# One issue order replaced by another: a 24,000-operation trunk with the list of its order and of its buffer slots drawn up anew

## The chip, the cores and the metric

One core of a Trainium2 chip. The metric is the device time of one execution in microseconds (us); shown are the median of three runs and one profiled execution. Five instruction streams matter: TensorE (PE: matmuls and transposes; PEld is its weight load), VectorE (DVE), ScalarE (ACT), GpSimd (POOL) and SyncE (SP, which issues the DMAs). Each takes its own instructions strictly in the order in which they were written, and a semaphore holds it where it needs another stream's result.

## The reference

One decoder layer on 2048 tokens of width 1024: a gated delta-rule mixer in chunks with 8 heads and 4 heads of cross-attention on 256 memory rows, an output projection, and a squared-ReLU MLP, each followed by a scaled residual and a layer norm.

```python
proj = x @ w_in                                   # q, k, v, z, a, b, mq
qkv = silu(causal_depthwise_conv(qkv, conv_w))
o = chunk_gated_delta_rule(l2_normalize(q), l2_normalize(k), v, g, beta)   # needs inv(I + lower) per chunk
o = rms_norm(o, gate_norm_w) * silu(z)
mix = concatenate([o, memory_attention(mq, mem_k, mem_v)]) @ w_out
x = layer_norm(ALPHA * x + mix, ln1_g, ln1_b)
x = layer_norm(ALPHA * x + square(relu(x @ w_ff1)) @ w_ff2, ln2_g, ln2_b)
```

## The kernel before

The tokens go in four blocks of 512, two blocks to a superblock. For each block `mixer` runs the eight heads: `dense` projects q, k and v (tiles `aq`, `ak`, `av` in PSUM, 128x512, 24 matmuls each, because every product is made of three fp32r products of high and low halves), applies convolution and SiLU; `gate` does z (`az`); `gdn_a` builds the decay matrices, inverts the unit triangular matrices (`invert`) and scales v; `gdn_b` runs the recurrence over four chunks of 128 (`pc`, `po`). The memory heads are `amq`, `sps`, `pmT`, `pmo`. After two blocks comes the output projection `out_seven` (`ao`), then `ff1` (`fA`, `fB`, `fC`) and `ff2` (`f2A`, `f2B`, `f2C`). These three are built as seven products of half matrices instead of eight, and stream their weights through `wraw` and `whl`. Between the superblocks stands `gate_seven` (`az` again). The large matmuls are fp32r; the small ones of `invert` and of the recurrence, and the transposes, are fp32.

The recorder `rec` collects 23,792 operations of all five engines as the code names them. `Recorder.issue` then writes them out in the order of the table `ORDER` (one list for all engines, kept compressed), and gives each buffer of eleven tags the physical place that the table `SLOT` names. So these two tables alone decide what stands ahead of what on each engine, and which earlier buffer a new one must wait for.

Three places of the code are spoken of below. The first is the end of `invert` and what follows it in `gdn_a`: PE multiplies `pp`, DVE and then ACT copy its two halves into `Y`, and PE transposes v into the same PSUM bank (`ptv`).

```python
pq = bank("pq", "ga%d" % par)[:, :P].rearrange("p (c f) -> p c f", c=2)        # from LP and YP
nc.scalar.copy(out=Q.rearrange("p (c f) -> p c f", c=2), in_=pq)               # "inv<-pq"
pp = bank("pp", "ga%d" % par)[:, :P].rearrange("p (c f) -> p c f", c=2)        # from X64 and Q
nc.vector.tensor_scalar_mul(Y3[:64, 2:4, 64:], pp[64:], -1.0)                  # DVE "Y<-pp"
nc.scalar.activation(Y3[:64, 0:2, 64:], pp[:64], AF.Copy, scale=-1.0)          # ACT "Y<-pp"
pv = trans(v3, "ptv")                                                          # PE, same bank
```

The second is the input of that `pp`: the tiles `inv` (X64, LB, LP and others in four fixed buffers), which DVE, ACT and POOL fill with small copies, while POOL also makes `dl` and `at` from `gb` by two `affine_select` of 128x512. The third is in `out_seven`: ACT copies the first product out of PSUM (`e<-ao`), and only then may PE use that bank again.

Of the kernel before, what the change touches and what calls it, by code (L numbers as in the profile page):

```python
# [10 lines left out]
AF = mybir.ActivationFunctionType  # L11
# [3 lines left out]
P = 128  # L15
TB = 512
NC = TB // P
D = 1024
KT = D // P
H = 8  # L20
MH = 4
M = 256
# [149 lines left out]
class Op:  # L172
# [4 lines left out]
    "c-oYm4YKPvj;uFiM~MIA{x|lRUxJiRbxpsS=$X2<k1R_R2?B{kV$AgUw*CL(8J}+&pS1rs_uJ36fAnsBzH|TcP5G0`r+m`ff6dSHNnM}z{Av3y"  # L177
    "{n3~Av1NSf(($?P|K@#c$)A1Dx9yYd&%UYDeYk$0mi=kdo0PMDpnblJzwICDb^r1CWIobGjL&}i&BbTlKmY8@YWv`<|D^p}`{;e#K5I&xB0c;w"
    "_L)Zc)P1VV&FJ_xKOC_?NKg4>UGP4<`ipv*_JxdnMLK$4@uzoP?%3lp+a89#U+g#g3q@yYX}_v#`uqFsK5^59)=&Qw-C3!1kLNyBF8VQk;`xk+"
    "0s1D!OkZ!l(mmAr!P1IHpne)(9{N8WwV%`eq__QBJTpG)ysTBnmd1nSgSpRA_aN{)&wfJt_`08b;nYRfUiJ`GeO&k73&&R-yH8V#hGsvJI`lg_"  # L180
    "8H2uWMAxo|oA)^jv!?Fh*`vGv_0N{&A<G(^tT$<ocG}+^%sOVt{xt84&-+2><j;Po$NL#sC)n4aSy6{CwXFSSpC~;V0L`%eY3oxoF>CF<65g%m"
    "+t)AEyhpF;ay4$cw~y{}-@yL*p0yggwa$-g=IgFCV{+3&+y9s2^`5l6*iSSkX3qZWqcbK=+p3w^bW3|B<jz`{e4>~7XK}vN{Wfd3-WN${<rnm&"
    "^^X^2zs|{L`uTW|P2M-S=M_(GU%O7#8C|Ud4j!H-k7oHEr+shz(fk`M@T^%n*Qe^v_tk53^jT)r?yH`jXIXP_pFTgn>aL|wpY<AveTZ&QPj&YA"
    "(mqf3xA*Pom-Nu{im8+v$LM+NKVxBZqs5kFf1dk#XSj?_yYJ)LzGYuR;a>NU=WTNIG*cQeeN!xxvX9kz-G?+k87+$3_eEs=eV?31wtus-bTktC"
    "ekPBEIpYT@%cl>EjF-kF#z)t&&sg;HWj5xw4%<UkY;Q17W#4HjF%WSpd9O=;RU^2ELUU6`R31!{jnTd6Yo%*NWQ^#3uCgxsBC;oR;X1YnsqrYE"
    "SU%?x_Y>C$=%0rV_VsJ@WIy-3Zmj60=P>v0l)~6OT18s(`~O+UMW#YFgEe0E1J)G7ChH`R|Bz(Ba?z*LlVoo&I<xnheGXaQZA<sn=&|bQY69ul"
    "to772V)4K4+&_u+({f~>FtR?a|0mme<|z+B&zRrdmPw|d$?|C->#wrw8uxGJS?zhctrli^&+DvbwC_b`pzOKcyni)K`K*nlY0ujm9Jct;Y-S8F"
    "Xu7SmO+e8c+CQ&tpwxRS|Ng&yxAXUHPRz@F0WvkL@wTs6L$G9=mj|(*<Lmq%PhGfZ7K|)Fm$}-j#G{_H>~*1icJAoYWxe}i57y-JFtZ))jjCvU"
    "?q{bZT3Lg8I_zhN3$Pg4z2ES2`RB>BV?(su#=nn%cTpMhEUW%$n)5BJ)o5WKI+m;1GBj-odz?l-3sO%?2k4p`TaWCO+?T>XdzAC~{Z$st|L%WY"
    "Ph~&kGMBfS{Uf*`OdL-nxi-AjE`Wj3Eir}m5EpGCgYjtF3d&j(ycgN3rrZ8z=6#7xeH$*1SHb4-VLzXj^!Kr2tYn9@X7?_rd9wd4T(EZS_h!F3"  # L190
    "#{biDSnLIT4_4Q`<(1_KZaX8>RktzGcelmCHIxmJsm%Y|fg4>u#iMh|TJO=&Y}3Tlx$0g(C2@L<!1lkiqPC;A_cylJul`v~(7NvR??L41c-H$w"
    "4@bAEJzb-XD_KW;TP}d+{des9>+;s*)9H;aVIMeI^4n$X?<Z-Sox()Z647;X9{qjUrx<?5dZ%&Tj%^C7@H5n!6U>u^|EUvJ?O42h^jzgO6#dvX"
    "QCd^_Z0)JOv?n#q`MMXuVikL@)$65O&<jnYCOfJ(t>Df!KCy$Faqy}=MC}4aenDaj{PKERiS9)x)37&jnaI78+3NJcn$<7Lo+@pIv0rups(lR|"
    "u)W>AI+HxVSoCe5t1aE`UO5XVEnM&!rcT%5Ek6}I2fER=H<6CXk|F7M`!n1C?sc&_J+htoGnq3B_ge1jzDhl1ztf?a1LY>kJAO1pc#B)9Smx2}"
    "h>uu8#cw-?PH%Nk;-Kn>oU3nn&uw=2l;ViLFPm;RMrhyJU~}wU^AMA!lQbWm2zT_ieH9vYyB<APe;}_|-_n*pyo&QDeyZRk<aIwSE8(UUY+&LK"
    "`(d-Z%08mALuw?329!&ded4IKKbri)zM`S!@n}kC&AC+Md+%GR6L<KV|7>1ko3y<(Y5o)~rP7`_>6f9`9qtF)2fx+j(&LXkT_N7&scDd&;ZK)m"
    "eX?0t3Ie-b3VqK9j6LCHKYYD<;PZ(uYYR+XU+0v1*_aIS?z=V$9kc(;mozb-y%KWOv)PL#E_L5(BMR6fJsir(+&|j+DgmrEw?|<Po0)tuO?p|O"
    "rFo`3Y9H=V(!kZO<-FbzSaA_Uqu#j3!FRMO_Iev0ORcd-t65j3xhQ9KPp)helyDUJ-Bhp`*bJ;;VGFKuBM1qKLg$aJY_UpL_9`7VpwnL_BI2fG"
    "JBwC;ew`Df<K1Y#kr^c7?=l^u@#ERs5Vq!hyIPIw^B3#AT1{{5U8NGVmDmoy`o|mM7#L8Q8hLNL?fZWE)4b#CDVXKkXl`_dzTxT0<Zt_d!;mzo"
    "VjI}o^RPuNL^d2sw68~B{R?~cDTtN*!ZKz3n!*I_ZN-ti=I2U&*4}aXZGEfrV?|@Iw<Ol^o{4&DTAYh`HLSd@D{<N-BeRcPngW`oj82jT-Ih_K"  # L200
    "ptZ7(8neddEO@yaT_>p6G{Tk7)IU>pRJ%93@c!u~>>=$(B@3dz3N+B*wewcyM~|WEQ4i+279vMfZ5@Pii3yh;J;J>R?R{)BLL9;_rb9hCx|_ZS"
    "xX<aZm5_yZpHBSvotdTdkvA%f$-wMKyzDXWPgf;S#GuRoTx2SB8T-;Ik24ea>XtR69EIQ7v}%?SkE&&)uuOxw<e9WRq7}qS;Wujp?4+~fJm=&U"
    "&}pwHxxhFcMRs)m_>#x8fVlRsG)3N;N-~|LD8|r=l3yVoJn0D#;Fa+E`aWUbvm;|)Yau)(vftyf#}qgAt9Yh^lB~dY?v}M0wrJtq%Tdu|X~`ye"
    "+fr>?y5qg8R=(O78{IyB>5pu1YXl^t=iRXyOyad~M}evaLVp?oziflBWR3wy<}@n9L0YSNu6e}x?Sp05bTvHnm5shJT^mCdKdc9}M^?*QD^d?$"
    "b3oUsGgJZ=JsyRf^8fVtSK)$OAw9^i4YP(4OQ=|->w;5a+@?1vjW+|IaLD$4qj~YwcI%&$o!lEZ*riac?PPTVDOQ-~2p(H^xUT)Cf+;QmWy>Rs"
    "BRDJD^#HR>`|DMPAl2jT&AXjGnxcaVo8@+f-!dLQEDe8S%GegP>SOMU<h8m@B#?mK7OkhOJ7`ZpWp<nl(Q>AgKr5D<OPQA*1F3kb0~kE9K`k5^"
    "9G3a#@5F%F@8q-S#S+Hw$W`z7FuLt3>pQpEnh&;eo0S}kjT2}?{>*wpdYivTR!L6zUWF6Op-`$%Z-hxdKKALR-{EnMZ3rAGI&9n%6ELfTt&U6p"
    "tP>BAmuzI@#D3aL2sw;0#8dBkeOEjU#Zw*7^GO(B2B0gD*Q9>mEL)DghXTNld9&}Hiy5HY!#6ng44I&%aT8--=)@Aqhr<ikEVi`<>6I-5P!s0K"
    "Mk{ml)ijpvZ8JMqVZ98^iWPf+oy6F)_MccU_MEDnv5y9H|MKG(bI%=Fc5Ijc5p8OFW$)|OQyzP^tj9i*-tFhL_t15~u)UC{w)%Zh0Nwy>dtTQ*"
    "0@2uZqK?3=nq#tkMSGTLo@?RgV_DL#PNciT{@?54C)pK}=YqgvnQ87+AGAkdLF~_3*!zVcj(z^T1F3C)wEp#GU99DQ3l=OK8Gn0Uxt5f+ISpHT"  # L210
# [336 lines left out]

SLOT = {
    ("sp", "iv"): (
        "30212130130223103102213002312130"  # L550
    ),
    ("tp", "tt"): (
        "0246135702173546413650274310657201345210670514637240153647023165743061470265730154761243754052367150"
# [1661 lines left out]
```

## Time and profile before

| | us |
|---|---|
| median of 3 runs (lowest to highest) | 2703.33 (2702.78 to 2704.77) |
| profiled execution, its own time | 2706.16 |
| its span, first to last instruction | 2704.4 |
| PE busy | 2686.8 |
| DVE busy | 2152.1 |
| ACT busy | 1645.0 |
| POOL busy | 392.4 |

The profiled execution is 2.8 us above the median and 1.8 us above its own span. "Busy" of PE is the time in which at least one matmul record is open; records overlap, so PE counts as busy through a wait that is shorter than the tail of the record before it. Starts are therefore read where spacings matter. Names are those of the program with buffer numbers left out; since all recorded operations are written out by one call, they all carry line L678 (L700 in the changed kernel, whose tables are 22 lines longer).

### The profile page before, as it was taken

How to read it: one execution, taken by the hardware profiler on the slowest of the kernel's cores; microseconds unless marked ns; L12 is line 12 of the kernel's file. 1: busy time of each engine (PE TensorE's matmuls, PEld its weight loads, DVE VectorE, ACT ScalarE, POOL GpSimd, SP SyncE). 2: the span in 40 equal slices, each digit the busy share in tenths (PEclk: the TensorE clock that was granted, in tenths of full speed). 3: DMA queues.
4: the chain of work that ended last, by engine and by line, in shares of the span. 5: the costliest groups of instructions: out<-in, count | busy, mean ns of one | idle time of the engine just before them, and what ended most of it. 6: DMA issues, size and time to landing. Idle time of an engine off the chain costs nothing.

```text
span 2704.4 us, 42512 instructions
## 1 busy us (share of the span) xinstructions
PE 2686.8 (99%) x13553; PEld 2245.9 (83%) x13553; DVE 2152.1 (80%) x5726; ACT 1645.0 (61%) x4132; POOL 392.4 (15%) x927
## 2 busy tenths in 40 slices
PE   9999999999999999999999999999999999999998
PEld 7888888888888888888888888888888888888887
DVE  7999889998877776766778988999978666567475
ACT  7778767786575555334446777777756655544341
POOL 3222223221000000000013222232201000000010
PEclk9999999999999999999999999999999999999999
DMA  8767558877788888889686444544578654486673
GB/s 310 249 226 268 188 185 296 294 262 258 277 300 292 303 289 289 295 286 299 236 285 210 140 149 156 188 157 157 207 267 280 226 175 148 152 291 216 208 245 113
DMA packets 223473, 633.74 MB, mean 234 GB/s; under 512 B 25712, under 2 KB 34832, under 8 KB 204304
## 3 DMA queue, kind: packets, MB, share of 16 engines
q1 hardware_dynamic: 222816, 630.97, 67.8%
q8 instruction: 107, 1.75, 0.3%
q14 instruction: 118, 0.97, 0.1%
q10 hardware_dynamic: 432, 0.05, 0.0%
HBM read 446.83 MB, written 184.09 MB: 233 GB/s over the span
## 4 chain that ended last, share of the span: by engine, by line
PE 87%; DVE 8%; DMA 2%; ACT 1%; issue 1%; POOL 0%; SPq 0%; POOLq 0%; DVEq 0%; ACTq 0%
PE fA L678 12%; PE f2A L678 11%; PE ao L678 8%; PE f2C L678 6%; PE fC L678 6%; PE aq L678 5%; PE av L678 5%; PE ak L678 5%; PE az L678 5%; PE f2B L678 3%; PE fB L678 3%; PE pc L678 3%; PE amq L678 3%; PE po L678 2%; PE pkq L678 1%
## 5 line engine op out<-in xcount | busy, mean ns | idle before, releaser
L678 ACT CAST whl<-wraw 128x512 fp32r<-128x512 f32 (+2 forms) x298 | 226.0, 769 | 200.8 <-PE fC L678 57.6
L678 DVE TENSOR_TENSOR whl<-wraw,whl 128x512 fp32r<-128x512 f32 (+2 forms) x298 | 256.9, 873 | 98.6 <-ACT whl L678 96.5
L678 PE MATMUL fA<-B,whl 128*128 128x512 f32 x1152 | 292.8, 389 | 0.0
L678 PE MATMUL f2A<-whl,X 128*128 128x512 f32 x1152 | 266.3, 389 | 0.2 <-DVE X L678 0.2
L678 PEld LDWEIGHTS f2A<-whl,X 128*128 128x128 f32 x1152 | 216.1, 188 | 45.8 <-DVE X L678 1.1
L678 PEld LDWEIGHTS fA<-B,whl 128*128 128x128 f32 x1152 | 216.1, 188 | 45.3 <-ACT hB L678 0.2
L678 PE MATMUL av<-T,whl 128*128 128x512 f32 x768 | 228.7, 405 | 1.0 <-ACT T L678 1.0
L678 ACT CAST X<-X 128x1024 fp32r<-128x1024 f32 x118 | 123.3, 1050 | 168.1 <-DMA X<-xsc 126.9
L678 PE MATMUL ak<-T,whl 128*128 128x512 f32 x768 | 220.8, 402 | 0.0
L678 PE MATMUL aq<-T,whl 128*128 128x512 f32 x768 | 216.6, 401 | 0.2
L678 DVE TENSOR_TENSOR X<-X,X 128x1024 fp32r<-128x1024 f32 x118 | 143.5, 1221 | 81.6 <-ACT X L678 81.4
L678 PE MATMUL fC<-B,whl 128*128 128x512 f32 x768 | 199.6, 390 | 0.2 <-DMA whl<-wfs 0.2
L678 PE MATMUL az<-T,whl 128*128 128x512 f32 x624 | 180.0, 402 | 0.0
L678 PE MATMUL f2C<-whl,X 128*128 128x512 f32 x768 | 177.8, 389 | 0.0
L678 PEld LDWEIGHTS fC<-B,whl 128*128 128x128 f32 x768 | 143.9, 188 | 31.0 <-DVE hs L678 0.6
L678 PEld LDWEIGHTS f2C<-whl,X 128*128 128x128 f32 x768 | 144.2, 188 | 29.9
L678 ACT CAST whl<-whl 128x1024 fp32r<-128x1024 f32 x92 | 96.7, 1052 | 117.7 <-DMA whl<-tsc 77.5
L678 PEld LDWEIGHTS aq<-T,whl 128*128 128x128 f32 x768 | 139.7, 189 | 26.0 <-issue 0.8
L678 POOL TENSOR_SCALAR ve<-mv 128x1 f32<-128x1 f32 x34 | 17.4, 512 | 981.9 <-DVE mv L678 981.9
L678 PEld LDWEIGHTS ak<-T,whl 128*128 128x128 f32 x768 | 139.7, 189 | 24.0
L678 PEld LDWEIGHTS av<-T,whl 128*128 128x128 f32 x768 | 138.4, 189 | 23.0 <-ACT T L678 1.3
L678 DVE TENSOR_TENSOR whl<-whl 128x1024 fp32r<-128x1024 f32 x92 | 112.0, 1220 | 49.6 <-ACT whl L678 49.2
(304 smaller groups left out, 6409.6 us busy)
## 6 DMA issues: line engine op xcount, KB each, us to landing
whl<-wsc SPq DMA_DIRECT2D x100, 1024.0 KB, 5.7
wraw<-in_w_ff_dram SPq DMA_DIRECT2D x106, 512.0 KB, 5.1
X<-xsc SPq DMA_DIRECT2D x96, 512.0 KB, 4.7
wsc<-whl SPq DMA_DIRECT2D x36, 1024.0 KB, 7.7
whl<-tsc SPq DMA_DIRECT2D x64, 512.0 KB, 4.6
xsc<-hB SPq DMA_DIRECT2D x96, 256.0 KB, 3.6
xo<-cat SPq DMA_DIRECT2D x80, 256.0 KB, 4.7
wraw<-in_w_in_dram SPq DMA_DIRECT2D x33, 512.0 KB, 4.8
```

The costliest lines, as they stand in the source:

```text
L678: o.fn(*[res(a) for a in o.args], **{k: res(v) for k, v in o.kw.items()})
```

## The change

Both tables are replaced. The operations, their number, shapes, engines and operands stay as they are. The new list was found by a search in which the durations of VectorE and GpSimd instructions were drawn at random from those traced, and the slots were listed anew for it. The diff is 855 lines of packed tables; the first lines of each show its kind:

```diff
 SLOT = {
     ("sp", "iv"): (
-        "30212130130223103102213002312130"
+        "31020321231002310132310231023102"
     ),
```

On every engine nearly all rows move by a few places. Three places show it. The first is DVE in the first superblock, block 1, the head whose `ptv` starts at 414.8 us in the profile: from the copy of `YP` (an input of the step) to `Y<-pp`; `wk` and `wraw` are weights of `ff1` being prepared, `cq` is the convolution of q, `Bc` and `Xc` belong to the inversion of another head, `inv<-dl` too. Before:

```order
L678 COPY YP<-Y 64x128
L678 COPY inv<-dl 32x2x32
L678 TENSOR_TENSOR Xc<-Xc,Bc 128x40
L678 TENSOR_TENSOR wk<-wraw,wk 128x512 x2
L678 STREAM_SHUFFLE Bc<-Xc 128x4
L678 TENSOR_TENSOR wraw<-wraw 128x512
L678 STREAM_SHUFFLE Bc<-Xc 128x44
L678 SCALAR_TENSOR_TENSOR cq<-raw,cw,cq 128x512
L678 TENSOR_SCALAR Y<-pp 64x2x64
```

And now:

```order
L700 COPY YP<-Y 64x128
L700 TENSOR_TENSOR wk<-wraw,wk 128x512 x2
L700 SCALAR_TENSOR_TENSOR cq<-raw,cw,cq 128x512
L700 TENSOR_TENSOR wraw<-wraw 128x512
L700 TENSOR_SCALAR Y<-pp 64x2x64
```

The four wide operations stay between the two, and four small ones have left. On PE four 128x512 matmuls stand between `pp` and `ptv` there, before and now.

The second is DVE at the last head of the second superblock, which runs inside the output projection (`f`, `xl` and `whl` are of `out_seven`, `cat` of the mixer's output). Before:

```order
L678 COPY cat<-pmo 128x512
L678 TENSOR_TENSOR cat<-cat 128x512 x2
L678 TENSOR_TENSOR f<-ao,e 128x512 x2
L678 TENSOR_TENSOR cat<-cat 128x512
L678 TENSOR_TENSOR xl<-xl,xh 128x512
L678 TENSOR_TENSOR whl<-whl 128x1024
L678 TENSOR_SCALAR Y<-pp 64x2x64
```

And now:

```order
L700 COPY inv<-inv 32x2x32 x2
L700 TENSOR_TENSOR cat<-cat 128x512
L700 TENSOR_TENSOR xl<-xl,xh 128x512
L700 TENSOR_TENSOR whl<-whl 128x1024
L700 TENSOR_TENSOR f<-ao,e 128x512
L700 TENSOR_SCALAR Y<-pp 64x2x64
```

Of the two `f` ahead of `Y<-pp` one has moved behind it, and the rest come earlier against PE: between `pp` and `ptv` PE now has 6 matmuls `ao` where it had 21.

The third is ACT shortly before that, at the last of the four copies `e<-ao` of this superblock. Before:

```order
L678 ACTIVATE pr<-pr,rc 128x256
L678 CAST X_23549<-X_23477 128x1024
L678 COPY Y<-ZT_23508 32x4x32
L678 CAST pm<-pmT 128x512
L678 COPY e<-ao 128x512
```

And now:

```order
L700 ACTIVATE pr<-pr,rc 128x256
L700 COPY e<-ao 128x512
L700 CAST X_23555<-X_23477 128x1024
L700 CAST pm<-pmT 128x512
```

The copy `e<-ao` has moved ahead of the two casts, `X` and `pm`, that stood before it.

More of the change, by code (lines that the diff above doesn't have):

```diff
@@ L182 @@
[L182 to L186, printed above, removed]
@@ new lines @@
+    "y|Q})pLOrH>Eas)9-n=WdzLP%=;r$Uy>63}-C;TR7`t&=?&*Hz9{--|zTc0pR98Pf{pd1uoQJEL43b_<9q9f$^hVd$bxW<@QxyhM<F&Z^J0@M@"
+    "IL>GI47%rgl6Ev!_qX?pl}Dt5+#?SiWiIaAH*x>hH9EZy{=Dbwca$}je0DTMThF_%?$3H}`abV9-qUOS_`cRf-yx~{-bB>{*VDe&&!G2n&v~!^"
+    "Z=Cz+7dO~G=N{w!N7JEf9q$g|zQ5eMB0ZANJ!!i)tE=yNwD*Kfqf{Rr)_tfaF6CbCz4v<W?S9zxp`LH!1otlf?w6`=P3LKMYSw3H1|IH@neyCU"
+    "4@O+qelPxhX>hnl)4e{Lc6U18x4DFIZ}#4rru!WPPa<x-7EMpDl>4>&{q^Ya-S3wk?~LO=w50kIZ*F~mKlc{3Ubfy{A3f-;dDWg8?=-HIziWQY"
+    "f9UvKt6+KIX^k}v%N@+oe4TYMnLG(JcQm?pXzJ4O?~PZ@T0NAh$yK|alAh-sfTmH?ENMkgLU(iTt<F1ZZ5|%(nMK|ijm}bQ8jbi+1Ko2zH=W@="
@@ new lines @@
+    ")vAYB8SQ&7UV0CIFoyS{G@~c4?&EA4^v(5lEJ)QF_+VQ;{CfFDwJw@&`e+eoy8JEKCJv-0u0O`LK)(LJ`q8!edFuY!{gG~7%kh4>R(^PGU7dGi"
+    "tB$U9rYjin!0*GVr!iMoOaiW;#SL(gcd5#fX|>$5)O$_sUd~+}noRe@I}}=gJD2L8u5IbEThVmA_pkNEsOci^!P}g?&@#Js-Z90REUcRT4viKN"
+    "C)2|3p6*-A?B2?qqK{Up7A3!EIY*wDE-l7oaMpV{`aR2p0ns1#VR6#t>$^kC+|vf3ll0BN-O(JfwnO7^=j%P74AxzU+|cZ45$`GQ6ujrYx4({O"
+    "No$Ass{6h#G^{dG*KAkp>%ISW=UI7j`1-y1DN9`MGpMu0Lu6jEg7w4}J5JBv+($nvkNe)y(WQI-X;rlQ>sbyDQ)Az>=iFH^Wu@jl$He>=ZH!uX"
+    "*VHwQ-IU2^l^&l<Ke}V0kK>o)ngJQ+*|ccyx8v_2(^VOqyB_qddsp`XW25gO?p55O#fVlt-gXDR>nZlfvq)$8(^cG&*IXI*Fy%B`Q{K^YX_#rx"
@@ new lines @@
+    "L2p7JiY37_SG={O4$N9y0u5ag#9Jhcn~51aI&_Q^BBIz}>LOXPq~$DprN`_n6M0lZYm%-w@%o;~s7T37i@Z_}ghyP0RMxWUN^FY3hykaC%vgg!"
+    "?^NQTWSOd9c#VY{>;W6dEDYC92GfYjSxveUyLhoQXFnkfRbc{jV`;;LCDd$7lv|PKZZ7i%bQFL%T+Mv1P9=3dwE)~se$z0v+!H5jP3<qErfjo3"
+    "$Kl^;BSpVc9Pt;Ja3G!dLPb5IrZ^lDCaHG^-<Hi5Nu@ziHy|RpD=xTaMIOLecQrJXkP@hfJ~xy8M8zc&#yQMLVd(VC*r*;CR-vN1pUjD;%dW(<"
+    "ayq2npA`HN?ten?A9t0~&tV-UWQttShzmO0D`&Zkj+CZp)eM`)QK@2Tc8*DppepVH0Xt?Ipm3q0^VfJ((*(M00Uk3kspQaW<OKE%0hD8bhb#>;"
+    "y^HOq_K?|uQQJ^j1E<qOQs`2x9&%KD)>9qQx{k+FiVZ?<k>YP7*!RV!bqxtb<h4>QVA!JZmh47w&JeKJ!5pmC$HP~e)&RJJ2r?Wm9PlX-A4G)~"
@@ L545 @@
+    "-R&z6aB5c*s?9ZfmlbtPA&qo8Q0@jE+Y;L1k<~k^WnqTmaQH}^l}+OKJh;@IPG4G}hj12&1WRI`pvvci$S-F}IzXldPj0=oas{btDAi`(n%6_}"
+    ")Vi~l_&t%%*p*C>DupBQrj$3-{gn@&8S(u{Pa^Wlt!BJB>NC{3mqY<juCL0~E5A$@5V~kJwZk%2SA#f#lgn-MTDfc)VH`JXaq_(pE)RcWgYHO7"
+    "OyMZo-!lC_y`S~R-*ubEBh-j7k`|Z?ch)Ywj(?TA{`9YBLiK5Wy{^3n>e?Xr|NaF?GJ@U"
 )
@@ L566 @@
-        "320132013201320132013213021"
+        "2103213021320321023120132130201230213013201012301312020212303210132013021320231031202131203130123010"
+        "3231020313021302102310231203120312301320132013201320213021302130213021302130213021302103210321032103"
+        "2103210320131203120312301230320132103201323012011320310322301320310213032130210320120121302131202103"
+        "2302103203123010232103210321013021302130213021302130213021302130213021302130213021302130213021302130"
+        "213021032103210321032132013"
@@ L592 @@
+        "a43a243a422a432a34a2433a42a24332a4a3423a243a42a3243a42a324a342a4238109765a23140968a7251698407352a196"
+        "40832a71465938a20719458263a0792456180a1492378564a140732568041a96237459806a91472308a5196339745a280691"
+        "6021938754a156a47890320932156a47809132"
     ),
     ("tp", "raw"): (
[L594 to L595 removed]
+        "0101110110001011011010110110110010110101010110100010100101101001101010101010101010101010101001010100"
@@ L602 @@
+        "983b1c44764899312750dab8bd168c4a059328cda05347b691671b4328a9cd6b0527413a09b87165d230bac948167d205abb"
+        "98d31534c012967a8c4b6d32a756106b89dc4a01cd723b65b8dac049b81539726410bbac7ad82535d92204d9611ba04c3785"
+        "6ab8572975c7ab62d401389a38c01d546723b07416dc85a9ca8923b04176dc85a932"
     ),
```

782 lines of the change are left out of this document (390 added, 392 removed).

## The prediction

> **What bounds the kernel now.** I read the page first, then the chain of waits, the table by stretches, PE's waits, and the places where PE waited longest.
>
> ```profile
> span 2704.4 us, 42512 instructions
> PE 2686.8 (99%) x13553; PEld 2245.9 (83%) x13553; DVE 2152.1 (80%) x5726; ACT 1645.0 (61%) x4132; POOL 392.4 (15%) x927
> ```
>
> PE has a record open for all but 17.6 us of the span. No instruction is added or removed, so only time in which PE isn't at its pace can be won. Its pace stands in the chain, where it runs free:
>
> ```profile
> 2391.11 43.52 PE f2A L678 x192
> 2434.63 43.52 PE f2C L678 x192
> ```
>
> That is 43.52 / 192 = 226.7 ns from one 128x512 matmul to the next. Where the mixers run, PE starts later than its pace allows without showing idle time, so I worked from starts. The first of the 13,553 is at 1.19 us and the last at 2695.82 us, 2694.6 us apart (both rows stand further down). Charging every matmul the usual spacing of its kind (9,960 of 128x512 at 226.8 ns, the others from 60 to 122 ns a record, those of the gate 147), fitted over the whole trace, gives 2665.6 us. PE is therefore late by 29.0 us in all. By the same count 4.9 us of that arise in the first 10 us, about 5 us are changes of matmul kind (below), and some 19 us are waits. A table by stretches shows where:
>
> ```profile
> 400.00:450.00 50.00, 48.83 (x282) 40.84 (x281) 47.36 (x179) 38.98 (x134) 15.19 (x38) 1.00 0.87 307
> 850.00:900.00 50.00, 50.00 (x222) 41.40 (x221) 39.23 (x63) 27.07 (x49) 0.00 (x0) 1.00 0.85 295
> 1800.00:1850.00 50.00, 49.52 (x295) 42.12 (x294) 46.50 (x195) 36.69 (x131) 15.46 (x40) 1.00 0.50 178
> ```
>
> Columns are PE, PEld, DVE, ACT and POOL busy, then PE's granted clock. In the MLP (850 to 900) PE never waits. In the mixers DVE is busy 46 to 47 of 50 us, so an instruction that PE needs often stands in DVE's queue behind others. The Trainium skill ("Perfetto Trace Analysis", Identifying the Most-Contended Engine) calls matmul busy time a poor measure of the distance to the roofline and wants the share of weight loads instead. The trace agrees with its first half (29.0 us late against 17.6 us idle) and not with the second: by weight loads 458 us would be free, yet the stretch without a wait shows them at 41.40 of 50.
>
> **The waits that the change touches.**
>
> ```profile
> PE ptv L678 <- ACT Y L678: 2.3, 6, 0.7
> PE pp L678 <- ACT inv L678: 1.6, 2, 1.1
> PE ao L678 <- ACT e L678: 1.1, 1, 1.1
> ```
>
> These three are the largest in the mixers (total, times, longest).
>
> *The copy `e`.* PE, then ACT:
>
> ```profile
> 1977.60 0.50 PE L678 MATMUL ao<-whl,X 128*128 128x512 f32 x1 [1.12 <-ACT e L678]
> ...
> 1976.48 0.59 ACT L678 CAST pm<-pmT 128x512 fp32r<-128x512 f32 x1 [1.40 <-DMA xo<-cat]
> 1976.96 0.59 ACT L678 COPY e<-ao 128x512 f32<-128x512 f32 x1
> ```
>
> `e` stood behind the cast `pm`, and that waited 1.40 us for a store to leave the buffer that `pm` takes over. Now `e` is ahead of `X` and `pm`, so the 1.12 us of PE go. What is late next is `pm`: if its store is as late as before, the product with the transposed probabilities may make PE wait instead. I take -1.1 us, ends -1.4 and 0.
>
> *The one slow DVE copy.* PE, ACT, DVE and POOL around 583 us:
>
> ```profile
> 583.00 0.63 PE L678 MATMUL pp<-inv 128*128 128x64 f32 x4 [1.10 <-ACT inv L678]
> ...
> 582.60 0.27 ACT L678 COPY inv<-pq 128x128 f32<-128x128 f32 x1 [0.41 <-DVE inv L678]
> ...
> 581.10 1.41 DVE L678 COPY inv<-inv 32x64 f32<-32x64 f32 x1
> ...
> 581.24 0.63 POOL L678 TENSOR_SCALAR_AFFINE_SELECT at<-gb 128x512 f32<-128x512 f32 x1
> 581.82 0.63 POOL L678 TENSOR_SCALAR_AFFINE_SELECT dl<-gb 128x512 f32<-128x512 f32 x1
> ```
>
> The 64 copies of that kind look like this otherwise (shortest/median/longest, ns):
>
> ```profile
> L678 DVE COPY inv<-inv x64: 183/186/1411, 110.6 to 1983.2; 32x64 f32<-32x64 f32 x64
> L678 POOL COPY inv<-Z x128: 227/232/2244, 103.8 to 1975.9; 32x64 f32<-32x64 f32 x128
> ```
>
> So 1.41 us is 186 ns plus the two selects that ran meanwhile (2 x 0.63). In all, 55 DVE instructions of the trace take over 150 ns more than their median, 21.4 us together, 42 of them beside a select; POOL's copies stretch the same way beside DVE. This spread is what the new search drew from. One of the 55 made PE wait 1.1 us. In the new order the copy stands earlier (1.4 us of PE work ahead of `pp`, was 1.1), still near the selects. I take -1.1 us here, ends -1.4 and 0; and since the 64 selects stay, +0.4 us for one chance in three that another falls on PE's chain, ends 0 and +2.2 (two such).
>
> The skill ("SBUF — State Buffer", Who interferes with whom) says why: the two engines share a port pair, whoever issues first holds it for its whole instruction, and the other is blocked. The trace agrees in size (1411 - 186 = 1225 ns against 1259 ns of selects). By that rule a delay belongs to the pair that meets and not to chance, so draws at random cannot tell the search which meetings its order makes; that is the third rival below.
>
> *From `pp` to `ptv`.* At each of the 32 heads PE waits for DVE's `Y`, then ACT's `Y`. The head of 414.8 us:
>
> ```profile
> 412.62 0.55 PE L678 MATMUL pp<-inv 128*128 128x64 f32 x4
> ...
> 414.80 0.44 PE L678 MATMUL ptv<-ident,cv 128*128 128x128 f32 x2 [0.66 <-ACT Y L678]
> ...
> 413.38 0.74 DVE L678 SCALAR_TENSOR_TENSOR cq<-raw,cw,cq 128x512 f32<-128x512 f32 x1
> 414.15 0.29 DVE L678 TENSOR_SCALAR Y<-pp 64x128 f32<-64x128 f32 x1
> ...
> 414.48 0.27 ACT L678 ACTIVATE Y<-pp 64x128 f32<-64x128 f32 x1 [1.43 <-DVE Y L678]
> ```
>
> DVE came to `Y` only after `cq`. I took for each head the time from the last `pp` to the end of ACT's `Y` (this head: 1.97 us) and the matmuls that PE has in between (4 x 226.7 = 0.91 us). The stalled heads show PE late by the first less the second less 0.25 us; summed over 32 heads that is 4.5 us. In the new order PE's filling falls from 42.5 to 37.5 us over the heads, through four heads that had the most or nearly so (they lose 5.8 us); ten heads that waited have 3.2 us less DVE work between `YP` and `Y` (0.75 us less in the rows shown), while others have more (32 heads: 78.3 us to 73.5). If every `Y` came as late as traced, the new filling would make the sum 7.2 us, 2.0 of them at the last head, which goes from 21 matmuls to 6:
>
> ```profile
> 1988.12 1.22 DVE L678 TENSOR_TENSOR whl<-whl 128x1024 fp32r<-128x1024 f32 x1
> 1989.38 0.29 DVE L678 TENSOR_SCALAR Y<-pp 64x128 f32<-64x128 f32 x1
> ```
>
> There the wide `whl` has moved ahead in time and DVE should be free. Moving each head's `Y` by its change in DVE work gives 2.6 us if only the decreases tell and 8.1 us if the increases do as well. So -1.9 to +3.6; I take -0.8, nearer to the lower end, since at the heads where work was added `Y` had time to spare in DVE's queue.
>
> *What else moves.* PE leaves its fp32r matmuls for another kind 609 times instead of 567 by the two lists. A fit over the starts gives 9 ns for each such excursion: +0.4 us, ends 0 and +0.8. SP's loads of the first 15 us change places among themselves, the last two of the first tokens by up to three rows; PE starts like this, and ends like this:
>
> ```profile
> 1.19 4.21 PE L678 MATMUL warm<-ones 128*128 128x128 f32 x18 [1.19 <-POOL mhalf L765]
> 6.37 0.80 PE L678 MATMUL av<-T,whl 128*128 128x512 f32 x1 [0.98 <-ACT T L678]
> ...
> 2695.82 0.39 PE L678 MATMUL f2A<-whl,xl 128*128 128x512 f32 x1
> ...
> 2699.95 1.42 DVE L678 SCALAR_TENSOR_TENSOR y<-y,rs,l2kq 128x512 f32<-128x512 f32 x2 [0.46 <-POOL rs L678]
> ```
>
> The wait for the first token tile (0.98 us) depends on the first two loads, which keep their places: 0, ends -1 and +1. After the last matmul the chain through DVE and POOL is the same in both lists: 0, ends 0 and +0.3. The 12 us of waits that are left are many of under 0.2 us in the recurrence and at `pkq`, whose places I couldn't tell better or worse by counts: PE matmuls within 300 ns of their chain's earliest time are 268 before and 261 now. 0, ends -3 and +3.
>
> Sum: -1.1 - 1.1 + 0.4 - 0.8 + 0.4 = -2.2 us: 2706.2 becomes 2704.0 for a profiled execution, and 2703.3 becomes 2701.1 for the median, which lies 2.8 us lower.
>
> **Rivals.** *First, the waits largely vanish.* If orders that hold under drawn durations leave DVE's and POOL's lateness no way to PE, the whole 4.5 us at `ptv`, the two single waits (2.2) and a third of the other 12 us go: -10.7 + 0.4, about 2693. For it: 42 of 55 slow DVE instructions are of one cause that the draws contain. Against it: fillings of only 0.92 us or less between `pp` and `ptv` stand at 12 heads (before, 11), which leave nothing for a late DVE.
>
> *Second, slower: `ptv` becomes tight.* Heads lost spare filling. If DVE came to `Y` 0.2 us later than traced on the average, the formula gives 11.5 us in place of 4.5, +7.0; with the other terms (-1.4) the time is 2708.9. It decides from 0.2 us on. For it: DVE has 3 us free in 50 there. Against it: DVE's work between `YP` and `Y` sums to less.
>
> *Third, meetings of DVE and POOL.* By the lock a new order can put selects on the copies that PE awaits. If seven of the 64 did, at 1.1 us each, the time would be 2703.3 - 2.6 + 7.7 = 2708.4. Against it: one did so far.
>
> *Fourth, nothing the clock can tell:* the waits move and sum to the same, 2703.
>
> **Chances and range.** A difference under 0.2% (5.4 us) can hardly be told from none. My forecast, waits a little shorter, has 0.34 and the fourth rival 0.22, which with the small change of either sign makes 0.54 for the same (0.02 of the forecast's falls to faster). The first rival has 0.26, so faster is 0.28. The second has 0.12 and the third 0.06: slower 0.18. The likeliest case gives 2701.1 us, with its own ends at 2697 and 2706. The range for eight in ten reaches into the first rival, to 2693.5, and to the price of the third, 2708.5.
>
> **What the new profile would show.** `e<-ao` no longer ends a wait of PE near 1977 us; `pp` shows no wait of 1.1 us, or shows it at another head with a stretched DVE copy beside a select; `ptv` waits sum to about 2 us in the list of waits, none at the last head over 0.5. First to last matmul start should be 2692 us. I am wrong if a single wait above 2 us appears, if the first matmul on data starts later than 7 us, or if SP holds a weight load so long that PE waits in the MLP, where it doesn't now.

## The result and the profile after

| | before | after |
|---|---|---|
| median of 6 runs (us) | 2704.30 (2702.78 to 2704.91) | 2689.73 (2688.74 to 2692.40) |
| ratio, 95% interval | 1 | 0.9948 [0.9935, 0.9961] |
| first to last matmul start (us) | 2694.6 | 2678.3 |
| lateness of PE against its pace | 29.3 | 12.9 |
| of that in the first 10 us | 5.1 | 5.0 |

The changed kernel is 14.6 us faster, 0.52%. The prediction was 2701.1 with a range down to 2693.5: the right side of zero, but outside its range. (Lateness is counted as in the prediction; with the spacings of one table for all runs the kernel before comes to 29.3 us instead of 29.0. Lateness is that of one profiled execution: that of before took 2706.2 us, 1.9 above the median of its six runs, that of the changed kernel 2689.7, its median. So lateness falls by 16.4 us where the median falls by 14.6.)

The page of the changed kernel, then its stretches from 400, 850 and 1800 us (columns as in the prediction):

```profile
span 2687.9 us, 42510 instructions
...
PE 2677.4 (100%) x13553; PEld 2249.0 (84%) x13553; DVE 2138.8 (80%) x5726; ACT 1641.0 (61%) x4132; POOL 396.3 (15%) x927
```

```profile
400.00:450.00 50.00, 49.75 (x292) 42.09 (x291) 48.19 (x175) 40.95 (x143) 17.33 (x37) 1.00 0.84 295
850.00:900.00 50.00, 50.00 (x222) 41.23 (x221) 37.03 (x59) 24.39 (x43) 0.00 (x0) 1.00 0.90 309
1800.00:1850.00 50.00, 50.00 (x304) 43.41 (x302) 46.25 (x200) 37.77 (x137) 14.90 (x42) 1.00 0.46 164
```

PE goes from 282 to 292 matmul records in the 50 us from 400 and from 295 to 304 in those from 1800, with VectorE as busy as before (48.19 against 47.36, 46.25 against 46.50). The list of all waits of PE has shrunk to three lines (total, times, longest), two of them in the first 10 us:

```profile
PE warm L700 <- POOL mhalf L787: 1.2, 1, 1.2
PE ak L700 <- ACT whl L700: 0.7, 1, 0.7
PE ptv L700 <- ACT Y L700: 0.4, 2, 0.2
```

The place of the copy `e`, PE and then ScalarE:

```profile
1960.55 2.30 PE L700 MATMUL ao<-whl,X 128*128 128x512 f32 x9
...
1959.61 0.58 ACT L700 COPY e<-ao 128x512 f32<-128x512 f32 x1
1960.08 1.07 ACT L700 CAST X<-X 128x1024 fp32r<-128x1024 f32 x1
1961.03 0.61 ACT L700 CAST pm<-pmT 128x512 fp32r<-128x512 f32 x1
```

Nine `ao` run on without a gap, and `pm` no longer waits for a DMA. The head that had the slow copy at 583 us, and the 64 copies of that form:

```profile
576.79 0.55 DVE L700 SCALAR_TENSOR_TENSOR Lc<-Lq,half,Lc 128x64 f32<-128x64 f32 x1
577.23 0.64 POOL L700 TENSOR_SCALAR_AFFINE_SELECT dl<-gb 128x512 f32<-128x512 f32 x1
577.38 0.50 DVE L700 TENSOR_TENSOR Bc<-Bc,Lc 128x4 f32<-128x4 f32 x1
577.48 0.63 PE L700 MATMUL pp<-inv 128*128 128x64 f32 x4
...
579.51 0.66 PE L700 MATMUL ptv<-ident,cv 128*128 128x128 f32 x4 [0.19 <-ACT Y L700]
```

```profile
L700 DVE COPY inv<-inv x64: 183/186/644, 110.1 to 1970.8; 32x64 f32<-32x64 f32 x64
```

The longest copy is 644 ns instead of 1411, and `pp` doesn't wait; the selects now meet `Lc` and `Bc`, which are stretched in its place and make `ptv` 0.35 us late. The head of 414.8 us is now that of 411.9:

```profile
410.20 0.55 PE L700 MATMUL pp<-inv 128*128 128x64 f32 x4
...
411.25 0.29 DVE L700 TENSOR_SCALAR Y<-pp 64x128 f32<-64x128 f32 x1
...
411.90 0.66 PE L700 MATMUL ptv<-ident,cv 128*128 128x128 f32 x4 [0.17 <-ACT Y L700]
```

From `pp` to VectorE's `Y` it was 1.53 us and is 1.05. The first matmul on data starts at 5.71 us (6.37 before), after fewer warm-ups and with the same lateness over the first 10 us; the tail after the last matmul is 8.2 us before and 8.1 after:

```profile
5.71 0.79 PE L700 MATMUL ak<-T,whl 128*128 128x512 f32 x1 [0.75 <-ACT whl L700]
...
2683.44 1.41 DVE L700 SCALAR_TENSOR_TENSOR y<-y,rs,l2kq 128x512 f32<-128x512 f32 x2 [0.46 <-POOL rs L700]
```

**Where the time came from.** For each of PE's 12,471 operations I compared when PE was free (the start before it plus its spacing) with the end of the last instruction of another queue that it awaits (inputs and reused buffers). A *late start* is one whose producer ended later. Beyond the first 10 us there are 50 of them before, worth 14.3 us, and 9 after, worth 1.7. The three starts right behind each late one add 3.6 and 0.5. That is 15.7 of the 16.3 us by which lateness beyond 10 us fell (24.2 to 7.9). VectorE's instructions more than 150 ns over their median, though, number 55 before and 57 after (21.4 and 20.9 us): the disturbance is still there, and little of it reaches PE. About 6 of the late starts before, worth 2.3 us, await a buffer whose place `SLOT` names (about 3 after, 0.3 us); the others await data or a buffer that has only one place.

### The profile page after: what moved, and what is told of

It reads as the page before. It is cut to its first block, busy times and chain, and to the rows that moved or that the text cites. A ratio compares the mean times of both kernels' runs of the same rounds, so it can differ in the third digit from the quotient of the medians.

```text
span 2687.9 us, 42510 instructions
## 1 busy us (share of the span) xinstructions
PE 2677.4 (100%) x13553; PEld 2249.0 (84%) x13553; DVE 2138.8 (80%) x5726; ACT 1641.0 (61%) x4132; POOL 396.3 (15%) x927
## 4 chain that ended last, share of the span: by engine, by line
PE 99%; DVE 1%; ACT 0%; DMA 0%; issue 0%; POOLq 0%; POOL 0%; DVEq 0%; SPq 0%
PE f2A L700 13%; PE fA L700 13%; PE ao L700 9%; PE aq L700 7%; PE av L700 7%; PE ak L700 7%; PE fC L700 6%; PE f2C L700 6%; PE az L700 6%; PE fB L700 3%; PE f2B L700 3%; PE pc L700 3%; PE amq L700 3%; PE po L700 2%; PE pkq L700 2%; PE pp L700 1%
## 5 line engine op out<-in xcount | busy, mean ns | idle before, releaser
L700 PEld LDWEIGHTS ak<-T,whl 128*128 128x128 f32 x768 | 139.7, 189 | 24.9 <-ACT whl L700 1.0
```

What stands on the lines that cost most here:

```text
L700: o.fn(*[res(a) for a in o.args], **{k: res(v) for k, v in o.kw.items()})
```

## The experiments

My theory after the result (A): the new order keeps lateness of VectorE's and ScalarE's queues from PE at many small places. Its rivals: a few single places (D), fewer meetings of VectorE and GpSimd (B), an order that is better planned without regard to disturbances (E); others are named where they come up. All runs are listed here, against a before of 2704.3 to 2704.8 us in each set of runs; below them stands each with its edit. "Late" is PE's lateness beyond the first 10 us of the profiled run, then the late starts there with their sum, and VectorE's instructions stretched by over 150 ns. That execution lies within 3 us of its kernel's median, but for `b_dbl` (4.1 below) and `peB`, `peA` and `dveA` (3.2 to 7.3 above); where the two disagree, the median counts.

| kernel | median us | ratio to before, 95% | late us | late starts | stretched |
|---|---|---|---|---|---|
| before | 2704.3 | 1 | 24.2 | 50, 14.3 | 55 |
| after | 2689.7 | 0.9948 [0.9935, 0.9961] | 7.9 | 9, 1.7 | 57 |
| h_ab | 2698.1 | 0.9979 [0.9970, 0.9988] | 15.8 | 25, 7.7 | 60 |
| h_ba | 2695.4 | 0.9966 [0.9952, 0.9979] | 13.8 | 30, 6.9 | 54 |
| b_nosel | 2696.6 | 0.9971 [0.9960, 0.9983] | 16.1 | 30, 8.6 | 4 |
| a_nosel | 2688.1 | 0.9940 [0.9927, 0.9952] | 5.9 | 7, 1.1 | 8 |
| b_dbl | 2725.1 | 1.0074 [1.0061, 1.0086] | 41.0 | 71, 30.4 | 96 |
| a_dbl | 2699.1 | 0.9980 [0.9971, 0.9988] | 17.3 | 31, 9.9 | 101 |
| b_e | 2704.3 | 0.9999 [0.9990, 1.0008] | 24.9 | 54, 15.2 | 55 |
| b_st | 2703.7 | 0.9996 [0.9988, 1.0005] | 24.2 | 51, 14.8 | 55 |
| b_ste | 2704.2 | 1.0001 [0.9992, 1.0010] | 26.5 | 52, 17.1 | 55 |
| a_unst | 2690.8 | 0.9951 [0.9938, 0.9965] | 9.0 | 12, 2.5 | 58 |
| b_rep | 2704.1 | 0.9997 [0.9988, 1.0006] | 22.6 | 47, 12.7 | 55 |
| b_rep2 | 2705.1 | 1.0002 [0.9993, 1.0011] | 24.5 | 37, 15.6 | 54 |
| b_relief | 2701.9 | 0.9991 [0.9982, 1.0000] | 24.2 | 48, 14.0 | 56 |
| peB | 2803.0 | 1.0367 [1.0352, 1.0382] | 130.6 | 124, 95.7 | 55 |
| peA | 2825.8 | 1.0449 [1.0435, 1.0463] | 147.1 | 169, 111.0 | 50 |
| dveA | 2844.4 | 1.0519 [1.0504, 1.0533] | 165.9 | 179, 122.9 | 46 |
| alt_a | 2707.2 | 1.0006 [0.9997, 1.0014] | 25.4 | 44, 15.5 | 53 |
| alt_b | 2700.0 | 0.9982 [0.9974, 0.9991] | 19.2 | 34, 11.3 | 60 |

### Where in the program

Two lists spliced at an operation up to which both have issued the same set:

```diff
-ORDER = before
+ORDER = after[:10200] + before[10200:]     # h_ab
+ORDER = before[:10200] + after[10200:]     # h_ba
```

> The changed list and its slots up to the middle of the first MLP (1042 us), where both lists have issued exactly the same operations, and the old list from there on. By the traces PE's lateness fell by 7.6 us before that point and by 8.4 us after it. Theory A (the gain is many small waits, spread over both mixers): about 7 us under before, 2697, and the first half's lateness as in the changed kernel. Theory D (a few single places, the largest of them the copy e and the last head near 1980 us, both in the second half): 2 to 3 us under before, 2701.

> The reverse: the old list up to 1042 us, the changed one from there on. Theory A: about 7 us under before, 2697, so that the two gains add up to the whole 14. Theory D: nearly the whole gain lies here, 2692 to 2693. If something global (the end, the start, the slots) decides, the two do not add up.

-6.2 and -8.9 us: 15.1 together, against 14.6 for the whole. The gain is spread over both halves and adds up, as theory A expected; theory D is out.

### The selects of GpSimd

```diff
-affine_select(out=dl3, in_=gb3, ...)                        # and at3
+affine_select(out=dl3[:, :, :8], in_=gb3[:, :, :8], ...)
-activation(dl3[:, c], dl3[:, c], AF.Exp, bias=gc, scale=-1.0)
+activation(dl3[:, c], ones, AF.Exp, bias=gc, scale=0.0)
```

> The old list with the disturbance taken away: the 64 selects of GpSimd write 8 columns per chunk instead of 128, and ScalarE's exponentials after them read a constant with scale 0 (the decay and the mask are left out of dl and at, every instruction keeps its place). Theory A1 (PE waited because DVE and POOL meet and the old order had no room for it): DVE's stretched instructions fall from 55 to about 13 and the time to 2692 to 2696. Theory E (the old order's waits stand with undisturbed durations too; the new one is simply better planned): 2700 to 2704, with the stretched instructions gone all the same.

> The changed list with the same selects narrowed. Theory A1: the changed order already absorbs the meetings, so 2688 to 2690, at most 2 us under the changed kernel, and the gap to the old list with narrowed selects closes to 3 to 6 us. Theory E: 2688 to 2690 as well, but the gap stays 11 to 14 us. Theory B (the new order has fewer or cheaper meetings; already doubtful, 57 stretched DVE instructions against 55): also 2688.

In the old list with narrow selects, GpSimd's select and the 64 copies of VectorE look like this:

```profile
L659 POOL TENSOR_SCALAR_AFFINE_SELECT dl<-gb 128x32 f32<-128x32 f32 x32 | 12.6, 394 | 33.1 <-DVE Bc L659 13.4 <-DMA gb<-scr 10.0 <-DVE R L659 4.7
```

```profile
L659 DVE COPY inv<-inv x64: 183/187/266, 110.2 to 1973.9; 32x64 f32<-32x64 f32 x64
```

Stretched instructions fall from 55 to 4. (In before 51 of the 55 overlap a select in time, where the prediction counted 42.) The old list gains 7.7 us, the changed one 1.7, and the gap between them shrinks from 14.6 to 8.6, between the 3 to 6 of A1 and the 11 to 14 of E. So by the medians, each known to some 3 us, the wide selects account for about 6 us of the gain, and about 8.6 us stay without them: each theory holds in part. The traces say the same: in before, 16 of the 50 late starts (5.7 us) have a stretched instruction in the 4 us of chain ahead of them, 34 (8.6 us) have none. There the awaited instruction stood behind others of ordinary length. That the two numbers agree doesn't show that the same starts are meant, and with narrow selects `dl` and `at` also come earlier.

The opposite, each select issued twice:

```diff
+                if "pattern" in o.kw:
+                    o.fn(*[res(a) for a in o.args], **{k: res(v) for k, v in o.kw.items()})
                 o.fn(*[res(a) for a in o.args], **{k: res(v) for k, v in o.kw.items()})
```

> The old list with each of the 64 selects dl and at issued twice over (same output, so 64 more GpSimd instructions of 0.63 us beside VectorE). From the run with narrow selects the meetings cost the old order about 6 to 8 us: with twice as many, 6 to 10 us above before, 2710 to 2714. If selects matter only through their meetings with a few copies that PE awaits: 2 to 4 us above.

> The changed list with the selects issued twice. Theory R (the new order leaves room between producer and consumer, whatever the lateness comes from): it loses clearly less than the old list does, 1 to 4 us, 2691 to 2694. Theory T (it was fitted to the meetings that occurred in its own durations): it loses as much as the old list or more, 2696 to 2700, with the 1.65 us of late starts beyond the first 10 us growing to 8 or more.

The largest waits of PE, old list and then changed list:

```profile
PE pp L661 <- ACT inv L661: 3.4, 5, 1.2
PE ptv L661 <- ACT Y L661: 3.4, 4, 2.2
PE aq L661 <- DVE z L661: 2.3, 1, 2.3
```

```profile
PE ptv L682 <- ACT Y L682: 1.7, 5, 0.7
PE pq L682 <- DVE Xp L682: 0.7, 1, 0.7
PE pkq L682 <- DVE at L682: 0.4, 1, 0.4
```

+20.6 against +9.3 us, each known to some 3 or 4 us. Theory R holds only in its ranking: 41 and 44 further stretched instructions cost the changed list about half as much. Its time of 2699.1 us and its late starts of 9.9 us lie where theory T put them. Both sizes were too low, and the changed list isn't immune: `dl` and `at` also come 0.6 to 1.3 us later there, which these runs don't separate from the meetings.

### The copy `e`

```diff
 # ScalarE, old list            # SyncE, old list
-COPY e<-ao (behind pm)         -load X1<-xo (ahead of the two stores)
+COPY e<-ao (ahead of X0, Y, pm)+load X1<-xo (behind the two stores xo<-cat)
```

Left alone is `b_e`, right alone `b_st`, both `b_ste`; `a_unst` puts the load ahead of the three stores in the changed list.

> The old list with one instruction moved: the copy e near 1977 us stands ahead of the casts X0 and pm and the copy Y on ScalarE. By the trace of before PE starts 1.29 us late there. If the copy was simply behind the others (the prediction's term): 1.1 to 1.3 us less lateness, 2703 in the median, nothing late next. If pm's store then holds up the product with the transposed probabilities: 0 to 0.5 us less, with a new wait at pmo.

With `e` alone it is on time, and `pm` is late next; PE, then ScalarE:

```profile
1976.69 0.66 PE L659 MATMUL pmT<-ident,pr 128*128 128x128 f32 x4 [0.66 <-DVE pm L659]
...
1975.32 0.59 ACT L659 CAST pm<-pmT 128x512 fp32r<-128x512 f32 x1 [0.63 <-DMA xo<-cat]
```

The 1.29 us at `e` became 0.83 at `pmT`, and lateness as a whole didn't fall. `pm` waits for a store of `cat`, and that store stood on SyncE behind a load which held the queue for 3.5 us until PE freed a buffer. The queue and its wait in before, then the queue after:

```profile
SPq L678 <- PE ao L678: 3.5, 1, 3.5
```

```profile
1965.02 0.32 SPq L678 DMA_DIRECT2D xo<-cat  x1
1968.92 0.32 SPq L678 DMA_DIRECT2D X<-xo  x1
1969.34 0.86 SPq L678 DMA_DIRECT2D xo<-cat  x2
```

```profile
1952.11 1.41 SPq L700 DMA_DIRECT2D xo<-cat  x3
1954.82 0.32 SPq L700 DMA_DIRECT2D X<-xo  x1
```

In before the stores go out 7.1 us ahead of `pm` (1976.48), after 8.9 us (1961.03).

> The old list with one DMA moved: on SyncE's queue near 1969 us the load of X1, which there holds the queue 3.5 us until PE has freed a buffer, goes behind the two stores of cat that stood behind it, as in the changed list. Nothing else moves; e stays behind pm on ScalarE. Theory S (the store, late behind that load, is what makes pm, e and PE late): the stores are issued about 2 us earlier, pm waits no longer for a DMA, and PE's 1.29 us at e are gone, 2703. If the order on ScalarE decides: PE is still more than 0.8 us late at e.

> The same move of the load and e ahead of X0, Y and pm on ScalarE, so both moves of the changed list at this place. Theory S: PE is on time at e and at pmT, as with the DMA alone. If both moves are needed: on time here and late in the run with the DMA alone.

> The changed list with the DMA move undone at this place: the load of X1 again ahead of the three stores of cat; e stays ahead of pm. Theory S: the stores are issued about 2 us later, pm waits for them, and PE comes late at pmT by up to 0.8 us, as it did where e alone was moved; the median within 1.5 us of the changed kernel, 2689 to 2691. If the store is early enough there anyway: no late start, 2689.7.

With the stores ahead, `pm` no longer waits for a DMA; in `b_st` the cast `X` ahead of it now waits for the load that was moved behind them:

```profile
1974.18 1.05 ACT L659 CAST X<-X 128x1024 fp32r<-128x1024 f32 x1 [1.17 <-DMA X<-xo]
1975.13 0.29 ACT L659 COPY Y<-ZT 32x128 f32<-32x128 f32 x1
1975.33 0.57 ACT L659 CAST pm<-pmT 128x512 fp32r<-128x512 f32 x1
1975.81 0.57 ACT L659 COPY e<-ao 128x512 f32<-128x512 f32 x1
```

Late starts here: 1.29 us before; 0.83 with `e` alone; 0.44 + 0.35 with the stores alone; 0.16 + 0.37 with both; none in the changed list; 0.66 there, at `pmo` behind `pm`, with the load put back. So theory S has the cause half: both moves count, and neither nor both together do what the whole order does. (That `b_ste` is later than before in all, 26.5 against 24.2 us, comes in good part from elsewhere: near 1415 us PE comes 1.9 us late to a matmul `av` behind a weight load, `whl<-wsc`, where before has no wait.) No median of these four differs from its list's by more than the interval.

### Mending single places

```diff
 # VectorE, one of 25 places (head of 414.8 us)
-SCALAR_TENSOR_TENSOR cq   (ahead of Y<-pp)
-STREAM_SHUFFLE Bc
 TENSOR_SCALAR Y<-pp
+STREAM_SHUFFLE Bc
+SCALAR_TENSOR_TENSOR cq   (behind it)
```

> The old list with 25 of its 50 late places beyond the start mended one by one, e not among them: at each, one to three instructions that stood just ahead of the late one on VectorE or ScalarE, and whose own readers come at least 0.5 us later, are put right behind it. They hold 6.4 us of lateness in the trace of before. Theory A (lateness is a matter of which few instructions stand ahead of the awaited one): 5 to 6.5 us under before, 2698 to 2699. Rival F (the order is tight as a whole; what is put behind makes PE wait elsewhere): at most 2.5 us under before, and new late places as many as those that went.

> A second round of mending single places: the list with 25 mended places, of whose late starts 22 more (4.4 us in its trace, most of them new in it, at pc behind VectorE's state and R) get the one or two instructions ahead of the late one put behind it. If mending converges: 3 to 4 us under the first round, 2700 to 2701. If lateness is handed on each time: 0 to 1.5 us, 2703 to 2704, and again some 20 new late places.

No gain, either time. At the 25 places 6.36 us of late starts fell to 0.96 in the first round, and 21 new ones of 4.46 us came up, nearly as many as rival F expected, about half of them in the recurrence behind VectorE's `state` and `R`. One of them at 491 us, in before and then with the places mended (VectorE, then PE):

```profile
489.78 0.70 DVE L678 SCALAR_TENSOR_TENSOR ck<-th,ck 128x512 f32<-128x512 f32 x1
490.61 0.35 DVE L678 SCALAR_TENSOR_TENSOR state<-state,el,pc 128x128 f32<-128x128 f32 x1
...
490.74 0.49 PE L678 MATMUL ptq<-ident,cq 128*128 128x128 f32 x3
491.06 0.43 PE L678 MATMUL pc<-state,ck 128*128 128x128 f32 x2
```

```profile
489.76 0.68 DVE L659 SCALAR_TENSOR_TENSOR ck<-th,ck 128x512 f32<-128x512 f32 x1
490.47 0.34 DVE L659 SCALAR_TENSOR_TENSOR state<-state,el,pc 128x128 f32<-128x128 f32 x1
...
490.12 0.49 PE L659 MATMUL ptq<-ident,cq 128*128 128x128 f32 x3
490.86 0.49 PE L659 MATMUL pc<-state,ck 128*128 128x128 f32 x2 [0.25 <-DVE state L659]
```

PE comes to `ptq` 0.62 us earlier than before, VectorE to `ck` 0.02 and to `state` 0.14. Here the lateness that was mended had been time that VectorE needed; without it PE runs into the next awaited instruction. Theory A, in the form that single instructions decide, falls. That the other new late starts come about in the same way, and not from what was put behind, isn't shown.

Less work for VectorE, at the same places in the queue:

```diff
-            sub(B[o], B[x], B[y])
+            nc.vector.tensor_tensor(out=B[o][:, :TB // 4], in0=B[x][:, :TB // 4], in1=B[y][:, :TB // 4], op=ALU.subtract)
```

> The old list with less VectorE work in one stretch: the 96 differences of weight quarters (wq, 0.68 us each, 24 of them between 317 and 620 us, the others in the first MLP, where PE never waits) work on 128 of 512 columns, so that three quarters of these sums are left out. About 10 us less of VectorE work lies in 300 to 620 us. Theory L (VectorE's queue is so full there that lateness is handed on from one awaited instruction to the next): PE's lateness between 300 and 600 us falls from 7.6 us to about 3.5, the second mixer keeps its 9, and the time is 2699 to 2701. If only the order of the instructions counts and not their load: at most 1.5 us less, 2703.

Lateness from 300 to 600 us falls from 7.6 to 4.4 us, near the 3.5 that the changed kernel has with all the work. VectorE's busy time there falls by 6.7 us (280.9 to 274.2), less than the 10 expected. The median, 2701.9 us, is 2.9 us below before with an interval that reaches a ratio of 1, and short of the 2699 to 2701 expected. In the profiled execution, which is the slowest of its 11 runs, the second mixer is 2 us worse. Counted from 1400 us on, half of that is one wait that before doesn't have: near 1412 us PE comes 1.1 us late to `av` behind that same weight load. (`b_rep2` and `alt_a` are late there, too, by 1.7 and 0.9 us.) The other half is open, so theory L rests on the stretch alone, in one trace.

### One queue from the other list

```diff
 PE      before            # peB: PE before, the others after, as near as PE allows
-others  before
+others  after             # peA and dveA likewise, with PE or VectorE fixed from after
```

> A list between the two: PE's instructions stand exactly in the old order, those of the other four queues in the changed order as nearly as PE's order and the buffers allow (a mean of 0.24 places off on VectorE and ScalarE; 1.8 and 2.0 places lie between old and changed). Theory Q (what the queues of VectorE and ScalarE hold ahead of an awaited instruction decides): near the changed kernel, 2690 to 2693. Theory P (what PE has to do between a matmul and its reader decides): near the old one, 2702 to 2705. Theory W (the queues are fitted to each other and lose the fit): 2704 or more, with more late starts than in either.

> The reverse: PE exactly in the changed order, the other queues in the old order as nearly as possible (0.25 places off on VectorE, 0.26 on ScalarE). Theory Q: near the old kernel, 2702 to 2705. Theory P: near the changed one, 2690 to 2693. Theory W: 2704 or more.

> VectorE exactly in the changed order, the other queues in the old order as nearly as possible (PE 0.34 places off, ScalarE 0.24). If VectorE's queue alone carries the gain: 2690 to 2695. If it takes ScalarE's queue too, or PE's: 2698 to 2705. Theory W: 2704 or more.

The three largest waits of PE with its own queue from the changed list and the others from the old one:

```profile
PE pc L644 <- DVE R L644: 13.5, 14, 3.6
PE pp L644 <- ACT inv L644: 7.6, 12, 2.2
PE pq L644 <- DVE YP L644: 4.6, 4, 1.7
```

+98, +121 and +140 us: theory W, and seven to ten times the whole gain. The two lists differ by only 3.1 places on PE and 1.8 on VectorE in the mean, but a queue of the one doesn't fit the queues of the other. No single queue carries the gain. How much of the loss comes from the simple way in which the other queues were filled in, or from the buffers, which got new places too, isn't separated.

### How long a piece is

```diff
-ORDER = before
+ORDER = pieces of after and before in turn, cut at 29 places   # alt_a; alt_b the complement
```

> The lists laced together: both are cut at the same 29 places, where the operations issued differ by at most six (20 to 80 us apart in the mixers), and pieces are taken in turn, the first from the changed list; buffers are placed anew by who came free first. By the traces the pieces taken from the changed list hold 6.8 of the 16.3 us. If an order counts within a piece of some 50 us, whole over all five queues: 5 to 8 us under before, 2697 to 2700. If the fit reaches farther than a piece (as single moved instructions and single queues suggest): no gain, or a loss at the 29 seams, 2704 and up.

> The complement, the first piece from the old list. The pieces from the changed list hold 9.5 us by the traces. If an order counts within a piece: 7 to 10 us under before, 2695 to 2698, and the two gains add up to the whole 14. Otherwise 2704 and up.

The whole is +2.5 and -4.8 us, -2.3 together: `alt_a` came out where the rival put it (2704 and up), `alt_b` between the two expectations. By stretches the reason shows. (Places are in PE's own pace here, lateness left out.) In the second mixer, 1412 to 1947 us, the six pieces of `alt_a` from the changed list hold 1.1 us of lateness (0.8 in the changed kernel, 4.0 in the old one), and the five from the old list 4.6 (4.4 in the old). There each piece of 20 to 65 us kept nearly what its own list gives it, and the two complements bear each other out: over the old list `alt_a` gains some 3 to 4 us there and `alt_b` 2.5, the changed kernel 5.5 to 7 (estimates from the starts; the bounds come from where the stretch is cut). In the first mixer it is so by half: 3.1 us in the new pieces (1.8 in the changed kernel, 3.9 in the old). In the MLP and the projections, where neither list loses much, the seams cost. In `alt_a` there are 2.9 us of lateness between 712 and 1000 us, where the old list has about 1.4, and 3.3 behind 2052, the largest part a single wait of a transpose. Of the 1.9 us between 1000 and 1412, 0.9 is the wait for the weight load named above, which kernels without seams have too. The transpose:

```profile
PE pt L668 <- ACT e L668: 2.5, 1, 2.5
```

So in the second mixer, and by half in the first, an order is good within a piece, for all five queues together, and a seam of two orders is dear in some places. This rests on one trace of each kernel.

## Why the prediction was wrong

- *What bounds the kernel* was right: PE's lateness was all there was to win, and 16.4 of its 29 us went. First to last matmul start was to be 2692 us and is 2678.3. Even with every term of the sum at its low end (-1.4, -1.4 and -1.9 for the three places, -1 and -3 for the start and the rest) it comes to -8.7 us, less than the 14.6 that were won.
- *The step that failed is "the 12 us of waits that are left", 0 ± 3.* Late starts apart from `ptv` and the two single places fell from about 8 us to under 1, and with them the starts right behind. Take `e` (1.3 us), the slow copy (1.3) and `ptv` (3.1) off, and about 9 of the 14.6 us in the median, or 10.7 of the 16.4 us of lateness, are left for this term: it was put at nothing and is the larger part of the gain. I had judged them by how many matmuls stand within 300 ns of their chain's earliest time in the two lists (268 and 261), which is nearly no change. Measured against the producers' ends, late starts went from 50 to 9. The count on the list can't see the queue ahead of the producer.
- *From `pp` to `ptv`* was mis-sized, -0.8 with the low end -1.9. The late groups at these heads fell from 4.0 to 0.9 us, by 3.1. The step moved each `Y` only by the work between `YP` and `Y` and left the rest of VectorE's queue where it was traced. But VectorE came to `Y` 0.77 us behind `pp` in the mean of the 32 heads, where it had been 1.10; that PE's filling fell from 42.5 to 37.5 us cost nothing.
- *The copy `e`*, -1.1: the wait is gone, but not by the move that the step priced. The move alone gave nothing, because `pm` was late next, which the step named; what it overlooked is the store on SyncE, moved ahead of a blocked load.
- *The slow copy*, -1.1 and +0.4: as it came out, in part by luck, since the step gave no reason why a copy that still stood near the selects should escape them. `pp` doesn't wait, and another meeting makes `ptv` 0.35 us late at the same head. By the Trainium skill ("SBUF — State Buffer", Who interferes with whom) a VectorE instruction in a 2-port perf mode shares a port pair with GpSimd: whoever issues first gets it for the whole instruction, and the other blocks. No row here shows the mode, but the traces agree that a delay belongs to the pair that meets: in seven other kernels that keep this place of the old list the copy took 1407 to 1417 ns. Where the times ahead of it change, the delay changes: the same copy took 186 ns in `b_relief` and 814 in `b_dbl`, whose list is the old one. And by its row the copy starts at 581.10 us, 0.14 ahead of the first select, and is held through both, so the row doesn't show that the one which starts first goes through.
- *Start and end* at 0 were right (5.1 to 5.0 us and 8.2 to 8.1). Changes of matmul kind, +0.4, can't be separated.
- *The rivals.* The first came nearest, 2693 at 0.26; it gave "a third of the other 12" where nearly all went. The second asked for VectorE to be later at `Y`; it was earlier. The third's meetings number 57 against 55 and stayed off PE's path but for the 0.35 us above. The fourth is out: 14.6 us are far beyond the interval.
- *The signs of being wrong* didn't appear: no single wait above 2 us, the first matmul on data at 5.71 us, no wait in the MLP. All three looked for a slower kernel, none for one in which more waits go than the sum had.

The mechanism, as far as shown: in the mixers VectorE is busy 46 to 48 of 50 us, and the runs suggest that in the old list PE's waits were the time in which it caught up. Mending single waits brought up others; less VectorE work made waits go from 300 to 600 us; whole pieces of the new list, all queues together, made them go with the same work in the second mixer. What the search did inside such a piece to let VectorE keep up isn't shown, nor whether drawn durations were needed for it rather than just more searching. That the new list loses about half as much to doubled selects would fit the draws, and as well a list that simply has fewer tight places. The slot table by itself, and GpSimd's own stretched copies (182 and 190, about as many in both), weren't tried; of PE's own late starts few await a placed buffer, but what the slots do to the other queues is open.

## What to carry to other kernels

Where an engine that feeds PE is as busy as VectorE here (46 to 48 of 50 us), don't count on mending PE's waits one by one: a wait may be paying the other engine's time, and here 5.4 us taken away at 25 places brought 4.46 us back at others. Judge a new order by how many consumers start after their producers ended, queue by queue, not by the dependence chain; and change all queues of a stretch together. When an instruction moves ahead of a blocked one, follow what the blocked one waits for onto the DMA queue, too.

## What the hardware showed beside that

In the first 10 us PE's pace differs from run to run with the same instructions. In `b_nosel`, whose list starts like the old one, 18 warm-up matmuls took 3.64 us (4.21 in the prediction's row), and the first on data shows 0.50 us instead of 0.80:

```profile
1.19 3.64 PE L659 MATMUL warm<-ones 128*128 128x128 f32 x18 [1.19 <-POOL mhalf L746]
6.42 0.50 PE L659 MATMUL av<-T,whl 128*128 128x512 f32 x1 [1.60 <-ACT T L659]
```

The granted clock is 1.00 in both traces there. It makes up to 2.0 us of difference between runs, so lateness is compared beyond 10 us.
